# First two channel tiles' shift and scale by TensorE, and x loaded first, in a planned encoder layer

## Chip, cores, metric

One Trainium2 chip, one of its cores. The metric is the device time of one execution in microseconds (us): the median of the runs shown.

## What is computed

One encoder layer on x of 512 x 2048, in float32. A conditioning vector c gives six rows (shift, scale and gate for each half) through a 2048 x 12288 matrix `w_ada`:

```
c_act = silu(c)
sh1, sc1, gt1, sh2, sc2, gt2 = split(c_act @ w_ada + b_ada, 6)
h = rmsnorm(x, g_mix) * (1 + sc1) + sh1
proj = h @ w_in                                  # 2048 x 3072
y = concat(lru(proj[:1024]) * gelu(proj[1024:2048]), pool(proj[2048:])) @ w_out
x = x + gt1 * y
h = rmsnorm(x, g_ffn) * (1 + sc2) + sh2
x = x + gt2 * ((silu(h @ w_gate) * (h @ w_up)) @ w_down)
out = rmsnorm(x, g_final)
```

The change touches the first three lines: shift and scale of the first half, and the normalised, transposed x.

## The kernel before

The channels (2048) lie in 16 tiles of 128 partitions, the 512 frames along the free axis. x comes as 16 pieces of 128 frames x 512 channels (`xs`). ScalarE (ACT) squares each piece with a running sum; VectorE (DVE) and ACT make `rstd1` of the sums (`rstd_from`). Then ACT multiplies each piece by its rstd, TensorE (PE) transposes it in 128x128 blocks against the identity, and ACT copies the four blocks of a channel tile from PSUM into `xt[k]`. All 16 tiles are transposed in one loop, ahead of the rest of the program text.

Shift and scale of a chunk of channel tiles come from `ada_columns(which, k0, nk)`. The chunks are ADA_CHUNKS, tiles 0 and 1 alone, then seven pairs. SP loads the columns of `w_ada`, DVE multiplies each block by its entry of `c_act` and adds it up (`ada_fma`, 16 operations for a chunk), and a matmul of one column against ones sums over the partitions. DVE adds the bias from `cols_a` and writes `gs` (scale) and `sh` (shift). `shifted(k)` applies them on ACT and splits the result into a high and a low fp32r part, `h[k]`; ACT makes `hi`, DVE the difference `lo`. The projection follows with three matmuls for each product (hi.hi, hi.lo, lo.hi): six output tiles are held in PSUM (`held_job`, banks `acc`), the others are computed for tiles 0 and 1, 2 to 7 and 8 to 15 at a time (`group_job`, banks `mm`, of which there are two).

The order is not that of the text. A class `Program` records every operation, and `schedule` places them engine by engine after a cost model, by due times that `deadlines` derives; every engine and queue then runs its list in order. An operation with `lead` gets a due time ahead of all others, in the order of these numbers. Buffers come from pools: `blk` has 69 tiles of 128x512, `raw` six and `araw` four of 128x1024. `buffers` decides whether an operation may take a new one yet. Since every operation is issued from one helper, all have one line, L356 (L359 after the change), and are told apart by the names of their tiles: `araw<-in_w_ada` is a load of w_ada, `b<-araw,c_act,b` a multiply-add of `ada_fma`, `mm<-ones,b` the sum over partitions.

Of the kernel before, what the change touches and what calls it, by code (L numbers as in the profile page):

```python
# [36 lines left out]
class Program:  # L37
# [116 lines left out]
    def deadlines(self):  # L154

        at = 0.0
        users, order, serves = {}, {}, {}
        for op in self.ops:
            op["due"] = 1e9
            if op["q"] == "PE":  # L160
                op["due"] = op["nominal"] = at
                at += op["t"]
            for name in op["tiles"]:
                tag = self.tags[name]
                if name not in users and tag != "blk":
# [12 lines left out]
        for js in before:  # L178
            for j in js:
                behind[j] += 1  # L180
        latest, queued, held = [at + 50.0] * len(self.ops), {}, {}
        heap = [(-latest[i], -i) for i, n in enumerate(behind) if not n]
        heapq.heapify(heap)
        while heap:
            _, i = heapq.heappop(heap)
            op = self.ops[i := -i]
            q, due = op["q"], latest[i]
            tag = self.tags.get(op["w"][0][0]) if q == "SP" and op["w"] else None
            if tag in ("raw", "araw"):
                due = queued[tag] = min(due, queued.get(tag, 1e9) - 0.6)  # L190
            op["due"] = min(op["due"], due - op["t"] - (self.SLACK if not op["dma"] else self.SLACK_DMA if q == "SP" else self.SLACK_SUM))
            if q in ("DVE", "ACT", "SP"):
                t = max(op["t"], self.DMA_ISSUE) if q == "SP" else op["t"] * self.LOAD
                op["due"] = held[q] = min(op["due"], held.get(q, 1e9) - t)
            for j in before[i]:
                latest[j] = min(latest[j], op["due"])
                behind[j] -= 1
                if not behind[j]:
                    heapq.heappush(heap, (-latest[j], -j))
        for op in self.ops:  # L200
            if op["lead"] is not None:
                op["due"] = op["lead"] - 1e3 + 1e-4 * op["i"]

    def schedule(self):
# [22 lines left out]
        taken, last_use = set(), {}  # L227
        waiting, ready = [len(op["pred"]) for op in ops], [0.0] * len(ops)
        clock = {q: 0.0 for q in self.QUEUES.values()}
        dma_free, table, busy, port = 0.0, None, {}, 0.0  # L230
        start, left = [None] * len(ops), len(ops)
        pace = [op for op in ops if op["q"] == "PE"][::-1]
        shift, wide = 0.0, False
# [45 lines left out]
        while left:  # L279
# [4 lines left out]
            for (q, _), heap in lanes.items():  # L284
                now, tried = clock[q], []
                while heap and (wide or len(tried) < self.SCAN):
                    due, i = heapq.heappop(heap)
                    tried.append((due, i))
                    if q == "PE" and pace and ops[i]["nominal"] > pace[-1]["nominal"] + self.AHEAD:
                        continue  # L290
                    need, when = buffers(ops[i], now)
                    if when is None:
                        continue
                    t = max(now, ready[i], when, port if ops[i]["port"] else 0.0)
                    cand = (t, due + 2.0 * (ops[i]["table"] not in (None, table)), i, need)
# [21 lines left out]
                early[tag].append(place[name])  # L317
            start[i] = t
            if op["dma"]:
                issue = self.DMA_ISSUE if q == "SP" else self.DMA_BUILD  # L320
                clock[q] = t + issue
                dma_free = max(dma_free, t + issue + self.DMA_START - self.DMA_ISSUE) + op["t"]
                end = dma_free + self.DMA_LAND
            else:
                if op["table"] not in (None, table):
                    t, table = t + self.TABLE_LOAD, op["table"]
                    start[i] = t
                end = t + op["t"]
# [31 lines left out]
def hybrid_trunk(ctx: ExitStack, tc: tile.TileContext, a: dict, out: bass.AP):  # L360
# [58 lines left out]
    def rows_of(src):  # L419
        return src.rearrange("(r p) -> r p", p=P)  # L420

    rows_c = blk()[0:16, 0:P]
    nc.sync.dma_start(out=rows_c, in_=rows_of(a["c"][0]), lead=1)
    c_act = const.tile([P, KD], F32, name="c_act")
    tp = mmps()
    nc.tensor.transpose(out=tp[:, 0:16], in_=rows_c, identity=ident[0:16, 0:16])
    nc.scalar.activation(out=c_act, in_=tp[:, 0:16], func=AF.Silu)

    def param_columns(cols, rows, srcs, lead=None):
        r = 0  # L430
# [32 lines left out]
    for q in range(4):  # L463
        for t in range(NT):
            xs[t][q] = blk()
            nc.sync.dma_start(out=xs[t][q], in_=x2[t * P:(t + 1) * P, q * 512:(q + 1) * 512], lead=(0, 2, 4, 6)[q])
            ss = ss1[:, 4 * t + q:4 * t + q + 1]
            nc.scalar.activation(out=blk(), in_=xs[t][q], func=AF.Square, accum_out=ss)

    rstd1 = rstd_from(ss1, NT, after=sqrt_ready)  # L470
    xt = []
    for k in range(KD):
        ps = mmps("acc")
        for t in range(NT):
            if k % 4 == 0:
                nc.scalar.activation(out=xs[t][k // 4], in_=xs[t][k // 4], func=AF.Copy, scale=rstd1[:, t:t + 1])
            nc.tensor.transpose(out=ps[:, t * P:(t + 1) * P], in_=xs[t][k // 4][:, (k % 4) * P:(k % 4 + 1) * P], identity=ident)
        xt.append(blk())
        nc.scalar.activation(out=xt[k], in_=ps, func=AF.Copy)

# [25 lines left out]
    def ada_columns(which, k0, nk):  # L506

        nc_ = nk * P
        acc = blk()[:, 0:2 * nc_]
        nko = 512 // nc_  # L510
        for ko in range(0, KD, nko):
            w = nc.tile(pool, [P, 1024], F32, "araw", f"araw{next(ids)}").rearrange("p (s a b) -> p s a b", s=2, a=nko)
            for i in range(2):
                nc.sync.dma_start(out=w[:, i], in_=w_ada[:, ko:ko + nko, 3 * which + i, k0 * P:k0 * P + nc_],
                                  lead=5 if which + k0 == 0 else None)
            for i in range(nko):
                ada_fma(acc.rearrange("p (s b) -> p s b", s=2), w[:, :, i, :], ko + i)
# [187 lines left out]
    def pool_group(g):  # L705
# [485 lines left out]
```

## Time and profile before

| | |
|---|---|
| median of 3 runs | 1891.26 us (1891.05 to 1896.01) |
| profiled execution | 1895.01 us |
| its span, first to last instruction | 1893.1 us |
| PE busy | 1806.1 us, 95% |
| DVE busy | 1539.7 us, 81% |
| ACT busy | 936.4 us, 49% |
| moved by DMA | 429.97 MB, mean 227 GB/s |
| mean granted TensorE clock | 0.989 |

Times in the trace count from the first instruction. Matmuls overlap, so how far apart they start says more than their length. In the stretches, PEclk is the granted share of TensorE's clock (1.00 is 2.4 GHz, 0.5 is 1.2 GHz), and the DMA share is the mean busy share of the 16 DMA engines; since packets overlap it can pass 1.

### The profile page before, as it was taken

The numbers are of one execution on the slowest core, as the hardware profiler recorded it, in microseconds if no ns is written. First come the engines' busy times: TensorE is split into PE (matmuls) and PEld (weight loads), VectorE is DVE, ScalarE is ACT, GpSimd is POOL, SyncE is SP. The second block draws the span as 40 slices with busy tenths as digits, with TensorE's granted clock in tenths as the row PEclk, the third lists the DMA queues.
The fourth block names the chain that finished last, engine by engine and source line by source line (L and its number), as shares of the span: only waits on it lengthen the run. The fifth ranks groups of instructions, "written<-read, shape, count | busy, mean of one in ns | idle before, by whom it ended". The sixth has DMA issues, their size and how long they took to land.

```text
span 1893.1 us, 22786 instructions
## 1 busy us (share of the span) xinstructions
PE 1806.1 (95%) x8011; PEld 1473.2 (78%) x8011; DVE 1539.7 (81%) x1974; ACT 936.4 (49%) x1221; POOL 197.4 (10%) x192
## 2 busy tenths in 40 slices
PE   3899999899999999999999999999999999999996
PEld 2687877688887888888888788787887888888875
DVE  5898998889969878678787867877667887888888
ACT  7434684422377545454554544545445543333345
POOL 0000054500001111111111111111110000000011
PEclk9999999999999999999999999999999999999999
DMA  9999755499954778788868877876799765947566
GB/s 297 312 349 292 237 183 178 141 327 318 364 168 97 189 201 222 202 211 219 226 180 217 224 191 208 221 194 183 169 291 341 245 232 186 354 143 261 195 155 164
DMA packets 285763, 429.97 MB, mean 227 GB/s; under 512 B 20760, under 2 KB 119760, under 8 KB 285648
## 3 DMA queue, kind: packets, MB, share of 16 engines
q1 hardware_dynamic: 259408, 378.17, 59.9%
q0 software_dynamic: 26240, 50.34, 15.9%
q8 instruction: 63, 1.03, 0.2%
q14 instruction: 52, 0.43, 0.1%
HBM read 378.63 MB, written 49.81 MB: 226 GB/s over the span
## 4 chain that ended last, share of the span: by engine, by line
PE 64%; DVE 14%; DMA 9%; issue 8%; ACT 3%; POOL 1%; SPq 1%; ACTq 0%; DVEq 0%; POOLq 0%
PE acc L356 62%; DVE b L356 10%; DVE lo L356 4%; DMA araw<-in_w_ada 3%; PE mm L356 2%; ACT b L356 2%; DMA raw<-in_w_ada 1%; ACT hi L356 1%; DMA raw<-in_w_ffn_up 1%; DMA araw<-in_w_ffn_up 1%; SPq L356 1%; DMA araw<-in_w_ffn_gate 1%; DMA raw<-in_w_out 0%; DMA f<-b 0%; DMA raw<-in_w_in 0%
## 5 line engine op out<-in xcount | busy, mean ns | idle before, releaser
L356 PE MATMUL acc<-hi,b 128*128 128x512 f32 x4208 | 1271.4, 392 | 5.3 <-ACT hi L356 2.2
L356 PEld LDWEIGHTS acc<-hi,b 128*128 128x128 f32 x4208 | 789.6, 189 | 169.8 <-ACT hi L356 7.6
L356 PE MATMUL acc<-lo,b 128*128 128x512 f32 x2104 | 782.9, 393 | 4.4 <-DVE lo L356 4.3
L356 ACT ACTIVATE hi<-raw 128x1024 fp32r<-128x1024 f32 (+2 forms) x297 | 306.6, 1035 | 447.2 <-PE acc L356 362.5
L356 DVE TENSOR_TENSOR lo<-raw,hi 128x1024 fp32r<-128x1024 f32 (+2 forms) x297 | 356.1, 1202 | 148.4 <-ACT hi L356 144.1
L356 PEld LDWEIGHTS acc<-lo,b 128*128 128x128 f32 x2104 | 396.1, 189 | 91.5 <-DVE lo L356 10.9
L356 ACT ACTIVATE hi<-araw 128x1024 fp32r<-128x1024 f32 x264 | 279.7, 1060 | 283.1 <-PE acc L356 257.5
L356 DVE TENSOR_TENSOR lo<-araw,hi 128x1024 fp32r<-128x1024 f32 x198 | 241.5, 1220 | 58.2 <-ACT hi L356 57.5
L356 DVE SCALAR_TENSOR_TENSOR b<-araw,c_act,b 128x512 f32<-128x512 f32 (+1 forms) x315 | 232.0, 741 | 11.3 <-DMA araw<-in_w_ada 8.0
L356 DVE TENSOR_TENSOR b<-b,b 128x512 f32<-128x512 f32 (+4 forms) x318 | 194.3, 633 | 13.7 <-ACT b L356 11.3
L356 PE MATMUL acc<-b,hi 128*128 128x512 f32 x608 | 191.4, 400 | 5.0 <-ACT b L356 2.1
L356 ACT ACTIVATE b<-b 128x512 fp32r<-128x512 f32 (+2 forms) x223 | 128.6, 597 | 106.1 <-DVE b L356 64.9
L356 PEld LDWEIGHTS acc<-b,hi 128*128 128x128 f32 x608 | 115.9, 192 | 32.4 <-ACT b L356 4.3
L356 PE MATMUL acc<-b,lo 128*128 128x512 f32 x304 | 116.7, 398 | 2.5 <-DVE lo L356 2.5
L356 POOL DMA_DIRECT2D araw<-in_w_ffn_up x44 | 53.1, 1206 | 586.7 <-DVE lo L356 412.1
L356 ACT ACTIVATE b<-acc 128x512 f32<-128x512 f32 x142 | 82.1, 594 | 57.6 <-PE acc L356 42.6
L356 DVE SCALAR_TENSOR_TENSOR lo<-araw,hi 128x1024 fp32r<-128x1024 f32 x66 | 80.5, 1220 | 34.4 <-ACT hi L356 34.1
L356 DVE TENSOR_TENSOR araw<-araw,raw 128x1024 f32<-128x1024 f32 x88 | 106.7, 1219 | 0.8
L356 POOL DMA_DIRECT2D raw<-in_w_ffn_up x44 | 53.0, 1204 | 317.7 <-DVE lo L356 290.2
L356 DVE SCALAR_TENSOR_TENSOR araw<-araw,raw 128x1024 f32<-128x1024 f32 x66 | 79.9, 1219 | 6.9 <-DMA raw<-in_w_ffn_down 3.5
L356 PE MATMUL mm<-b,hi 128*128 128x512 f32 x192 | 62.1, 404 | 10.3 <-ACT b L356 10.3
L356 PEld LDWEIGHTS acc<-b,lo 128*128 128x128 f32 x304 | 58.5, 192 | 16.0 <-DVE lo L356 3.8
(72 smaller groups left out, 868.2 us busy)
## 6 DMA issues: line engine op xcount, KB each, us to landing
araw<-in_w_ada SPq DMA_DIRECT2D x256, 256.0 KB, 4.7
raw<-in_w_ffn_down SPq DMA_DIRECT2D x88, 512.0 KB, 5.3
f<-b SPq DMA_DIRECT2D x154, 256.0 KB, 3.7
b<-f SPq DMA_DIRECT2D x154, 256.0 KB, 6.0
araw<-in_w_ffn_gate SPq DMA_DIRECT2D x44, 512.0 KB, 3.8
raw<-in_w_ffn_up SPq DMA_DIRECT2D x44, 512.0 KB, 4.5
araw<-in_w_ffn_up POOLq DMA_DIRECT2D x44, 512.0 KB, 6.6
raw<-in_w_ffn_gate SPq DMA_DIRECT2D x44, 512.0 KB, 4.9
```

The lines of the kernel that those rows point to most:

```text
L356: getattr(getattr(self.nc, queue), method)(*args, **kw)
```

## The change

1. Tiles 0 and 1: `ada_scalars` takes the place of the multiply-adds. Each w_ada block is the stationary operand of a one-column matmul with `c_act`, 16 for the shift and 16 for the scale, adding up in PSUM. Four loads of 0.5 MB take the place of eight of 0.25 MB.
2. The rows of c, b_ada and the norms' gains are loaded from ACT's queue, not SP's. The planner counts them there.
3. x: the leads are 0, 2, 4 and 4.5 in place of 0, 2, 4 and 6, while tile 0's w_ada has 5; so all of x stands ahead of w_ada on SP.
4. `transposed(k)` makes one tile of `xt`, and the main loop calls it two tiles ahead of the chunk. For tiles 0 to 7 the moving operand is the identity times rstd (`diag`), a plain f32 matmul, and ACT does not scale x; for tiles 8 to 15 it stays as it was. The PSUM bank comes from `mm`, not `acc`.
5. The planner asks for buffers at the later of the engine's own clock and the latest start placed so far (`today`).

```diff
+XT_AHEAD = 2
+DIAG_TILES = 8
...
-                t = max(op["t"], self.DMA_ISSUE) if q == "SP" else op["t"] * self.LOAD
+                t = max(op["t"], self.DMA_ISSUE) if q == "SP" else self.DMA_ISSUE if op["dma"] else op["t"] * self.LOAD
...
-                    need, when = buffers(ops[i], now)
+                    need, when = buffers(ops[i], max(now, today))
...
+            today = max(today, t)
...
-    nc.sync.dma_start(out=rows_c, in_=rows_of(a["c"][0]), lead=1)
+    nc.scalar.dma_start(out=rows_c, in_=rows_of(a["c"][0]), lead=1)
...
-            nc.sync.dma_start(out=xs[t][q], in_=x2[t * P:(t + 1) * P, q * 512:(q + 1) * 512], lead=(0, 2, 4, 6)[q])
+            nc.sync.dma_start(out=xs[t][q], in_=x2[t * P:(t + 1) * P, q * 512:(q + 1) * 512], lead=(0, 2, 4, 4.5)[q])
...
-    for k in range(KD):
-        ps = mmps("acc")
+    diag = blk()
+    for t in range(NT):
+        ts(out=diag[:, t * P:(t + 1) * P], in0=ident, scalar1=rstd1[:, t:t + 1], scalar2=None, op0=ALU.mult)
+    def transposed(k):
+        ps = mmps()
         for t in range(NT):
+            tok, x = slice(t * P, (t + 1) * P), xs[t][k // 4]
+            if k < DIAG_TILES:
+                nc.tensor.matmul(ps[:, tok], x[:, (k % 4) * P:(k % 4 + 1) * P], diag[:, tok], start=True, stop=True)
+                continue
             if k % 4 == 0:
-                nc.scalar.activation(out=xs[t][k // 4], in_=xs[t][k // 4], func=AF.Copy, scale=rstd1[:, t:t + 1])
+                nc.scalar.activation(out=x, in_=x, func=AF.Copy, scale=rstd1[:, t:t + 1], after=xt[1])
...
+        if which == 0 and nk == 1:
+            return ada_scalars(k0)
...
+    def ada_scalars(k0):
+        ps = mmps()
+        for i in range(2):
+            for ko in range(0, KD, 8):
+                w = stage("araw", 8, P)
+                nc.sync.dma_start(out=w, in_=w_ada[:, ko:ko + 8, i, k0 * P:(k0 + 1) * P], lead=5 if k0 == 0 else None)
+                for k in range(8):
+                    nc.tensor.matmul(ps[:, i:i + 1], w[:, k, :], c_act[:, ko + k:ko + k + 1], start=ko + k == 0, stop=ko + k == KD - 1)
+        ada_end(0, k0, 1, ps)
...
     for ci, nk in enumerate(ADA_CHUNKS):
+        end = start + nk
+        for k in range(len(xt), min(KD, end + XT_AHEAD)):
+            transposed(k)
         ada_columns(0, start, nk)
```

What it does to the order, at three places. First, PE at the first projection matmuls, before (acc_138 and acc_140 are transposed tiles, acc_156 the first held output tile, b_171 and b_172 the two parts of channel tile 0):

```order
L356 MATMUL acc_140<-ident,b_97 128x128
L356 MATMUL acc_138<-ident,b_103 128x128
L356 MATMUL acc_140<-ident,b_99 128x128
L356 MATMUL acc_140<-ident,b_101 128x128
L356 MATMUL acc_140<-ident,b_103 128x128
L356 MATMUL acc_156<-b_171,hi_174 128x512
L356 MATMUL acc_156<-b_172,hi_174 128x512
L356 MATMUL acc_156<-b_171,lo_175 128x512
```

and now (mm_138 is a transposed tile with the diagonal b_118, mm_152 tile 1's shift and scale, acc_125 to 127 held output tiles):

```order
L359 MATMUL mm_138<-b_118,b_83 128x128
L359 MATMUL mm_152<-c_act,araw_153 128x1 x8
L359 MATMUL mm_138<-b_118,b_85 128x128
L359 MATMUL mm_138<-b_118,b_87 128x128
L359 MATMUL mm_152<-c_act,araw_154 128x1 x8
L359 MATMUL acc_125<-b_145,hi_148 128x512
L359 MATMUL acc_125<-b_146,hi_148 128x512
L359 MATMUL acc_125<-b_145,lo_149 128x512
L359 MATMUL mm_152<-c_act,araw_155 128x1 x8
L359 MATMUL acc_126<-b_145,hi_148 128x512
```

Before, 48 of the 64 transposes stood ahead of the first projection matmul; now 12 do, and the small matmuls of tile 1's first two loads stand there too.

Second, DVE ahead of `gs` of tiles 8 and 9, before (mm_355 is the sum for these tiles, b_406 the multiply-adds for tiles 14 and 15):

```order
L356 TENSOR_TENSOR lo_362<-raw_360,hi_361 128x1024
L356 SCALAR_TENSOR_TENSOR b_386<-araw_394,c_act,b_386 128x512
L356 SCALAR_TENSOR_TENSOR b_406<-araw_408,c_act,b_406 128x512
L356 TENSOR_TENSOR lo_365<-raw_363,hi_364 128x512
L356 SCALAR_TENSOR_TENSOR b_386<-araw_394,c_act,b_386 128x512
L356 TENSOR_TENSOR gs_154<-mm_355,cols_a 128x2
```

and now (mm_346 and b_405 in their places):

```order
L359 TENSOR_TENSOR lo_356<-raw_354,hi_355 128x512
L359 SCALAR_TENSOR_TENSOR b_385<-araw_393,c_act,b_385 128x512
L359 SCALAR_TENSOR_TENSOR b_405<-araw_406,c_act,b_405 128x512
L359 TENSOR_TENSOR b_188<-b_327,b_188 128x512
L359 TENSOR_TENSOR gs_123<-mm_346,cols_a 128x2
```

The `gs` stood behind the second w_ada load of tiles 14 and 15 (araw_408, the first is araw_407); now it stands behind their first (araw_406).

Third, PE at the second pooling group's first matmuls, before (mm_614 and mm_617 are its outputs, acc_624 a gate tile at channel tiles 12 and 13):

```order
L356 MATMUL acc_624<-b_398,hi_636 128x512
L356 MATMUL acc_624<-b_399,hi_636 128x512
L356 MATMUL mm_614<-b_603,hi_612 128x512
L356 MATMUL mm_617<-b_603,hi_612 128x512
L356 MATMUL acc_624<-b_398,lo_637 128x512
```

and now (mm_613, mm_616; acc_623 and 624 the same two gate tiles, at channel tiles 4 to 7):

```order
L359 MATMUL acc_623<-b_255,lo_630 128x512
L359 MATMUL acc_624<-b_229,lo_630 128x512
L359 MATMUL mm_613<-b_602,hi_611 128x512
L359 MATMUL mm_616<-b_602,hi_611 128x512
L359 MATMUL acc_624<-b_231,hi_629 128x512
```

The pooling matmuls stand 38 matmuls of 512 columns further up.

## Rows read from the trace of the kernel before

**Rows 1.** The page, parts 1 and 2: busy time; DMA in 40 slices.

```profile
PE 1806.1 (95%) x8011; PEld 1473.2 (78%) x8011; DVE 1539.7 (81%) x1974; ACT 936.4 (49%) x1221; POOL 197.4 (10%) x192
```

**Rows 2.** Stretches: busy time of each engine, clock, DMA share, GB/s.

```profile
core 0: us, PE busy (x) PEld busy (x) DVE busy (x) ACT busy (x) POOL busy (x), PEclk, DMA share, GB/s
0.00:10.00 10.00, 0.26 (x1) 0.18 (x1) 0.54 (x3) 6.50 (x14) 3.09 (x24) 1.00 0.70 212
...
40.00:50.00 10.00, 8.68 (x39) 5.77 (x38) 9.52 (x14) 10.00 (x20) 0.00 (x0) 0.83 0.92 286
50.00:60.00 10.00, 7.28 (x26) 5.25 (x27) 8.00 (x12) 2.00 (x3) 0.00 (x0) 0.89 0.93 298
...
130.00:140.00 10.00, 10.00 (x46) 8.28 (x45) 10.00 (x19) 3.25 (x5) 0.00 (x0) 1.00 1.05 370
...
150.00:160.00 10.00, 8.59 (x27) 6.84 (x28) 8.15 (x15) 6.15 (x11) 0.00 (x0) 0.66 0.85 276
...
250.00:260.00 10.00, 7.02 (x32) 5.53 (x31) 10.00 (x13) 9.91 (x12) 7.33 (x6) 1.00 0.73 239
```

**Rows 3.** Timeline of ACT: start, length, operation, count, idle time before and its releaser.

```profile
22.79 0.63 ACT L356 ACTIVATE b<-b 128x512 f32<-128x512 f32 x1 [5.98 <-DMA b<-in_x]
...
26.36 0.63 ACT L356 ACTIVATE b<-b 128x512 f32<-128x512 f32 x1
```

**Rows 4.** Timeline of SP's DMA queue.

```profile
5.13 0.97 SPq L356 DMA_DIRECT2D b<-in_b_ada  x2
...
8.71 2.37 SPq L356 DMA_DIRECT2D b<-in_x  x4
...
18.36 2.07 SPq L356 DMA_DIRECT2D b<-in_x  x4
...
83.21 2.94 SPq L356 DMA_DIRECT2D araw<-in_w_ada  x4
```

**Rows 5.** Timeline of DVE.

```profile
18.07 7.78 DVE L356 SCALAR_TENSOR_TENSOR b<-araw,c_act,b 128x256 f32<-128x256 f32 x15
...
29.25 0.15 DVE L356 SCALAR_TENSOR_TENSOR s<-s,s 128x4 f32<-128x4 f32 x1
...
92.40 1.40 DVE L356 SCALAR_TENSOR_TENSOR b<-araw,c_act,b 128x512 f32<-128x512 f32 x2
...
94.35 0.16 DVE L356 TENSOR_TENSOR gs<-mm,cols_a 128x2 f32<-128x2 f32 x1
...
146.41 0.75 DVE L356 SCALAR_TENSOR_TENSOR b<-araw,c_act,b 128x512 f32<-128x512 f32 x1 [0.85 <-DMA araw<-in_w_ada]
...
148.34 0.15 DVE L356 TENSOR_TENSOR gs<-mm,cols_a 128x2 f32<-128x2 f32 x1
```

**Rows 6.** Timeline of PE.

```profile
41.54 1.20 PE L356 MATMUL acc<-b,hi 128*128 128x512 f32 x2
...
97.38 1.43 PE L356 MATMUL acc<-b,hi 128*128 128x512 f32 x5
...
147.29 0.39 PE L356 MATMUL mm<-b,lo 128*128 128x512 f32 x1
151.41 2.92 PE L356 MATMUL acc<-b,hi 128*128 128x512 f32 x6 [1.68 <-ACT b L356]
...
154.99 0.63 PE L356 MATMUL acc<-b,lo 128*128 128x512 f32 x1
155.42 0.63 PE L356 MATMUL acc<-b,hi 128*128 128x512 f32 x1
```

**Rows 7.** Groups by form, 0 to 50 us (PE) and 78 to 148 us (DVE): busy, mean ns, idle.

```profile
L356 PE MATMUL acc<-ident,b 128*128 128x128 f32 x64 | 12.0, 340 | 5.6 <-ACT b L356 5.4
...
L356 PE MATMUL mm<-ones,b 128*128 128x1 f32 x8 | 1.6, 303 | 13.9 <-DVE b L356 13.9
...
L356 DVE SCALAR_TENSOR_TENSOR b<-araw,c_act,b 128x512 f32<-128x512 f32 x58 | 42.8, 747 | 1.9 <-DMA araw<-in_w_ada 1.8
```

**Rows 8.** Timeline of PE, later.

```profile
256.90 1.38 PE L356 MATMUL acc<-b,b 128*128 128x512 f32 x5 [2.98 <-DVE b L356]
...
379.33 0.79 PE L356 MATMUL mm<-b,hi 128*128 128x512 f32 x1 [4.30 <-ACT b L356]
```

More of the change, by code (lines that the diff above doesn't have):

```diff
@@ L229, in schedule @@
         clock = {q: 0.0 for q in self.QUEUES.values()}
-        dma_free, table, busy, port = 0.0, None, {}, 0.0
+        dma_free, table, busy, port, today = 0.0, None, {}, 0.0, 0.0
         start, left = [None] * len(ops), len(ops)
@@ L319, in schedule @@
             if op["dma"]:
-                issue = self.DMA_ISSUE if q == "SP" else self.DMA_BUILD
+                issue = self.DMA_BUILD if q == "POOL" else self.DMA_ISSUE
                 clock[q] = t + issue
@@ L427, in hybrid_trunk, with param_columns @@
     nc.scalar.activation(out=c_act, in_=tp[:, 0:16], func=AF.Silu)
-    def param_columns(cols, rows, srcs, lead=None):
+    def param_columns(cols, rows, srcs, queue, lead=None):
         r = 0
@@ L433, in param_columns @@
             n = src.shape[0]
-            nc.sync.dma_start(out=rows[r:r + n, :], in_=src, lead=lead)
+            queue.dma_start(out=rows[r:r + n, :], in_=src, lead=lead)
             r += n
@@ L471, in hybrid_trunk @@
     xt = []
-    for k in range(KD):
-        ps = mmps("acc")
+    diag = blk()
[3 more added lines that the diff above has]
+        ps = mmps()
         for t in range(NT):
+            tok, x = slice(t * P, (t + 1) * P), xs[t][k // 4]
+            if k < DIAG_TILES:
+                nc.tensor.matmul(ps[:, tok], x[:, (k % 4) * P:(k % 4 + 1) * P], diag[:, tok], start=True, stop=True)
+                continue
             if k % 4 == 0:
-                nc.scalar.activation(out=xs[t][k // 4], in_=xs[t][k // 4], func=AF.Copy, scale=rstd1[:, t:t + 1])
-            nc.tensor.transpose(out=ps[:, t * P:(t + 1) * P], in_=xs[t][k // 4][:, (k % 4) * P:(k % 4 + 1) * P], identity=ident)
+                nc.scalar.activation(out=x, in_=x, func=AF.Copy, scale=rstd1[:, t:t + 1], after=xt[1])
+            nc.tensor.transpose(out=ps[:, tok], in_=x[:, (k % 4) * P:(k % 4 + 1) * P], identity=ident)
         xt.append(blk())
@@ L513, in ada_columns @@
             for i in range(2):
-                nc.sync.dma_start(out=w[:, i], in_=w_ada[:, ko:ko + nko, 3 * which + i, k0 * P:k0 * P + nc_],
-                                  lead=5 if which + k0 == 0 else None)
+                nc.sync.dma_start(out=w[:, i], in_=w_ada[:, ko:ko + nko, 3 * which + i, k0 * P:k0 * P + nc_])
             for i in range(nko):
@@ L520, in ada_columns, with ada_end @@
             nc.tensor.matmul(ps[:, j:j + 1], acc[:, j * P:(j + 1) * P], ones[:, 0:1], start=True, stop=True)
+        ada_end(which, k0, nk, ps)
+    def ada_scalars(k0):
[7 more added lines that the diff above has]
+        ada_end(0, k0, 1, ps)
+    def ada_end(which, k0, nk, ps):
         b0 = which * 32 + k0
@@ L735, in hybrid_trunk @@
                   [b_ada[0:32, :], b_ada[48:80, :], rows_of(a["g_norm_mix"][0]), rows_of(a["g_norm_ffn"][0])],
-                  lead=3)
+                  nc.scalar, lead=3)
     start = 0
@@ L739, in hybrid_trunk @@
     for ci, nk in enumerate(ADA_CHUNKS):
+        end = start + nk
+        for k in range(len(xt), min(KD, end + XT_AHEAD)):
+            transposed(k)
         ada_columns(0, start, nk)
-        end = start + nk
         for k in range(start, end):
@@ L746, in hybrid_trunk @@
                           [a["w_conv"][0].rearrange("i (r p) -> (i r) p", p=P), rows_of(a["b_conv"][0]), rows_of(a["b_rg_a"][0]),
-                           rows_of(a["b_rg_i"][0]), rows_of(a["lru_lambda"][0]), a["ls_pool"][0].rearrange("g (r p) -> (g r) p", p=P)])
+                           rows_of(a["b_rg_i"][0]), rows_of(a["lru_lambda"][0]), a["ls_pool"][0].rearrange("g (r p) -> (g r) p", p=P)], nc.sync)
             sp, spn = softplus()
```

## Prediction, before the changed kernel ran

> **What bounds the kernel now.** I read the page first, then the stretches, then single engines. The page [rows 1] says TensorE (PE) is busy for 95% of 1893.1 us, so a change at the start can win only what PE loses there. The stretches [rows 2] show where: in 0 to 10 us PE does nothing (0.26 us), in 40 to 60 it is 87% and 73% busy at a granted clock of 0.83 and 0.89, in 130 to 140 it is full, in 150 to 160 it has 0.66 of its clock, and in 250 to 260 it is idle for 3 us. The reader is to see two more columns: DMA is at a share of 0.92 to 1.05 in the three stretches between 40 and 140, and VectorE (DVE) at 8.0 to 10.0 of 10 us. So once the projection runs, three things are nearly full at a time, and PE's early gain must be carried by the other two.
>
> Why PE starts late: ScalarE (ACT) takes its last Square of x at 26.36 us, since the last quarter of x landed so late (5.98 us of waiting at 22.79) [rows 3]; SP issued that quarter at 18.36, behind eight pieces of w_ada [rows 4]. rstd is ready at 29.40 [rows 5], and PE's first projection matmul comes at 41.54 [rows 6].
>
> Two places later decide what an early start is worth. Channel tiles 6 and 7 start on PE at 97.38 [rows 6]; their scale `gs` was written by DVE at 94.35, at the end of an unbroken run of DVE work whose last w_ada pieces were issued at 83.21 [rows 4, 5]. Tiles 8 and 9 start at 151.41 after PE finished its earlier work at 147.68: their `gs` stood in DVE's queue until 148.34, behind a fused multiply-add that waited 0.85 us for a w_ada piece at 146.41 [rows 5, 6]. That hole is followed by matmuls 0.43 us apart in place of 0.23 (154.99 to 155.42; five in 1.43 us at 97.38).
>
> **The change part by part.** The sum is made against the profiled execution, 1895.0 us (span 1893.1); the median of the runs is 1891.3, 3.7 us lower, and I carry the difference over to it.
>
> *x first, small rows on ACT.* Sixteen pieces of 0.262 MB are 4.19 MB. In 0 to 10 us DMA moved 212 GB/s at a share of 0.70, so some 300 GB/s when full [rows 2]: 14 us and 2 us to begin, 16 us. From the last Square to rstd is 3.0 us (26.36 to 29.40), so rstd stands at about 19 instead of 29.4. Five row DMAs now stand ahead of ACT's first Square; two such on SP took 0.97 us [rows 4], so 2.4 us, before any x has landed: nothing. The first rows took SP from 5.13 to 8.71, when the next x piece was issued [rows 4]: 3.6 us at most for the stream. The Trainium skill ("DMA: Bandwidth & Descriptors", Issuing engines are not separate DMA queues) speaks against more than that: DMAs of all engines run on the same 16 engines, and a second issuer saves issue time only. By that rule the moved rows win no bandwidth, and the sum by it is the one I use: 1.5 us, half of the 3 us that DMA stood idle in the first stretch (the other half is its start); ends 0 and 3.6.
>
> *Tiles 0 and 1 by PE.* DVE loses 2 x 16 multiply-adds, twice 16/15 of 7.78 us [rows 5], 16.6 us, and gains four 128x128 scalings. DVE was waiting for DMA there, so this is worth nothing by itself; it gives DVE slack until about 150. PE gains 64 matmuls of one column at up to 0.303 us and loses 4 [rows 7]: 18 us, nearly all in time when PE waits for the next piece. Only the last 8 behind a landing count, 2.4 us, against 0.5 us for DVE's last add: 2 us on a path that is now 9 us shorter. In the new order (the first above) PE also holds 16 of tile 1's small matmuls ahead of the first projection matmul, so that one waits for the sixth w_ada load: 9.45 MB by the order of SP, at 0.31 MB/us and 2 us, 32.5 us. **PE starts 9 us earlier** (28 to 36 by rates of 0.37 and 0.28).
>
> *What is late next.* Counted over SP's rows, the last w_ada piece of tiles 6 and 7 stands at 26.44 MB before and 26.38 MB now; for tiles 14 and 15 it is 50.43 and 50.37. The same bytes through a stream that is full: tile 6 cannot come 9 us earlier. Tile 8's `gs` is behind 45.97 MB before (the waiting piece at 146.41) and 45.39 MB now, as the second order above shows: 0.58 MB at 0.34 MB/us is 1.7 us, and 1.5 us from the start of the stream. So `gs` comes 3.2 us earlier by DMA, and 1.6 us more since DVE has less ahead of it than before (it ran from 146.41 to 148.34 behind that piece; I leave 0.3 us of the 1.9): **4.8 us**. PE itself would be there earlier still: from 97.38 it needs 216 matmuls of 0.2275 us, 49.1 us, nine of which are now done before tile 6, and tile 6 comes about 2 us earlier, 95.5; so it arrives near 145 and waits 1.7 us or so, where it waited 3.7. In 250 to 260 a hole of 2.98 us left the granted clock at 1.00 [rows 2, 8]; after the 3.7 us of 147.68 to 151.41 it was 0.66. A hole of 1.7 us should keep it: 13 matmuls x 0.20 us, **2.6 us**.
>
> *Transposes moved into the full stretch.* Before, all 64 were over by 46 us. Now they are made two tiles ahead: 16, those of tiles 12 to 15, come after tile 8 has started, when PE is full. PE was busy 12.0 us with 64 of them [rows 7], 0.19 each; **3.2 us lost** (2 to 5.4, the mean of one being 340 ns). The 32 with a diagonal of rstd are f32 matmuls of a shape that the trace lacks; between 0.19 and 0.43 (the 512-column matmul at the low clock) they cost up to 8 us more, but stand ahead of tile 6's and 8's gates, where PE waits: nothing.
>
> *DVE after 150.* By tile 14's `gs` DVE has passed 55.61 MB now and 54.10 before: six w_ada pieces, 4.5 us of multiply-adds at 0.747 us [rows 7] done ahead. In 240 to 260 DVE is full and PE loses 2.98 us behind it [rows 8]: I take 2 us back (0 to 3).
>
> Sum: -4.8 - 2.6 + 3.2 - 2.0 = **-6.2 us**, 1888.8 for the profiled execution, 1885 as a median.
>
> **The rivals.** *A, the whole start is kept.* For it: 286 and 298 GB/s in 40 to 60 against 370 in 130 to 140 [rows 2] look like a stream held back by its buffers and by DVE, and DVE is now lighter. At 350 GB/s 26.4 MB would be in by 77.5, not 89; then PE's own work sets the pace. It keeps 9 us of start, 2.6 of clock and 2 of DVE, loses 3.2: -10.4, 1881 (1876 to 1883). Against it: shares of 0.92 and 0.93. The skill's ceiling of about 358 GB/s for one core (same page, Specifications) would allow it: by that figure alone, an estimate, 26.4 MB need 74 us.
>
> *B, nothing arrives.* DMA's first hole is not closed, the clock falls after the wait at tile 8 as before, the transposes cost 5 us: -1.7 - 1.6 - 2 + 5 = about 0, 1891 (1887 to 1893). For it: three resources full at a time, equal bytes.
>
> *C, slower: the pooling matmuls.* The new order puts the four pooling groups' first matmuls 10, 38, 30 and 23 places earlier among the 512-column matmuls (the third order above shows the second group). PE is in order, and before the fourth group it already waited 4.30 us for an ACT split [rows 8]. If the pooled tiles come no earlier than the rest of the kernel, the second group stalls 38 x 0.2275 = 8.6 us, and one fall of the clock adds 2.6: +11.2 on -6.2, 1896. It decides from 6.2 us of stall on. Against it: ACT's splits of these tiles were placed earlier too, and POOL's and DVE's part was over well before.
>
> *D, part of it does nothing:* if the first projection matmul is not earlier than 38 us, the order of PE eats the start; this ends as B.
>
> **How the numbers follow.** A measurement here tells 0.3%, 5.7 us, from no change: faster is below 1885.6. My forecast has 0.36 (its own range 1881 to 1888.5), A 0.26, B with D 0.26, C 0.12. Faster: all of A and 0.23 of the forecast, 0.49; slower: nearly all of C and a little of B's end, 0.13; the rest 0.38. The likeliest time is 1885. The range takes A down to 1875 and most of C, up to 1895.
>
> **What would show it.** Right: ACT's last Square near 16 and rstd near 19; first projection matmul at 30 to 35; tile 6 at 94 to 97 and tile 8 at 145 to 148, each right behind a `gs`; no low clock near 150; DMA full from 3 us on. A shows as tile 6 before 90. C shows as PE waits for ACT of over 5 us between 290 and 380. The forecast is wrong if tile 8 starts after 150, or if the gain at tile 8 is not there at 260.

## The result, and the profile after

The changed kernel takes 1902.11 us (median of 5 runs, 1901.52 to 1909.11) beside 1891.83 us for the kernel before (5 runs on the same chip). The ratio is **1.0063, 95% interval 1.0042 to 1.0083**: slower by 0.6%, where 1885 was forecast. The profiled execution took 1901.52 us, its span is 1899.7 us, 6.6 us more than before.

The page's busy line [rows 1] shows PE with 26.7 us more work and DVE with 10.0 us less:

```profile
PE 1832.8 (96%) x8163; PEld 1502.1 (79%) x8163; DVE 1529.7 (81%) x1946; ACT 931.5 (49%) x1214; POOL 194.4 (10%) x192
```

The stretches of the changed kernel, with the columns of [rows 2]:

```profile
0.00:10.00 10.00, 0.65 (x2) 0.36 (x2) 0.80 (x4) 5.41 (x11) 2.13 (x23) 1.00 0.69 170
10.00:20.00 10.00, 1.14 (x6) 1.17 (x6) 0.58 (x4) 9.30 (x27) 0.00 (x0) 1.00 1.09 383
20.00:30.00 10.00, 10.00 (x49) 10.00 (x48) 3.92 (x11) 2.21 (x3) 0.00 (x0) 1.00 1.10 378
30.00:40.00 10.00, 9.31 (x50) 8.89 (x49) 1.59 (x5) 2.01 (x3) 0.00 (x0) 1.00 0.80 258
40.00:50.00 10.00, 10.00 (x47) 9.13 (x47) 0.00 (x0) 0.60 (x1) 0.00 (x0) 0.59 0.47 146
50.00:60.00 10.00, 10.00 (x39) 8.95 (x38) 4.71 (x9) 4.00 (x6) 0.00 (x0) 0.56 0.37 117
...
110.00:120.00 10.00, 10.00 (x33) 8.20 (x34) 9.08 (x28) 2.56 (x4) 0.00 (x0) 0.66 1.09 360
...
150.00:160.00 10.00, 9.72 (x44) 7.42 (x42) 9.88 (x20) 3.82 (x7) 0.00 (x0) 1.00 1.03 345
...
250.00:260.00 10.00, 10.00 (x45) 8.27 (x45) 9.23 (x13) 8.71 (x12) 5.74 (x6) 1.00 0.58 181
```

For the same stretches before, three rows are needed beside those of [rows 2]:

```profile
10.00:20.00 10.00, 0.39 (x1) 0.18 (x1) 2.43 (x6) 5.65 (x16) 0.00 (x0) 1.00 0.99 289
20.00:30.00 10.00, 0.99 (x4) 0.93 (x4) 8.21 (x27) 4.27 (x11) 0.00 (x0) 1.00 1.02 324
30.00:40.00 10.00, 8.26 (x47) 6.66 (x47) 7.78 (x18) 10.00 (x19) 0.00 (x0) 1.00 1.09 369
```

Summed over these columns, 1.1 MB more than before have come in by 30 us. The loss is behind that, most of it in 40 to 60 us. DVE does nothing at all in the first of these stretches (9.52 us before), DMA falls to 146 and 117 GB/s (286 and 298 before): 3.2 MB less have come in by 60 us, 10 us of a stream of some 0.3 MB/us. PE is shown busy throughout, at a clock of 0.59 and 0.56. What PE does there is in its timeline (start, length, operation, records in the run, idle time before):

```profile
18.86 12.08 PE L359 MATMUL mm<-c_act,araw 128*128 128x1 f32 x56 [12.26 <-DMA araw<-in_w_ada]
...
38.00 2.11 PE L359 MATMUL mm<-c_act,araw 128*128 128x1 f32 x16
39.98 0.69 PE L359 MATMUL mm<-b,b 128*128 128x128 f32 x4
40.51 2.23 PE L359 MATMUL mm<-c_act,araw 128*128 128x1 f32 x16
42.60 1.20 PE L359 MATMUL acc<-b,hi 128*128 128x512 f32 x2
43.60 0.63 PE L359 MATMUL acc<-b,lo 128*128 128x512 f32 x1
44.03 3.41 PE L359 MATMUL mm<-c_act,araw 128*128 128x1 f32 x16
...
50.00 3.41 PE L359 MATMUL mm<-c_act,araw 128*128 128x1 f32 x16
```

Each one-column f32 matmul leaves two records, so the eight of one w_ada piece are a run of 16: 3.41 us where the granted clock is 0.50, 2.11 and 2.23 us in the two runs that lie mostly where it is 1.00. At 1.00 the records start 0.112 us apart, at 0.50 0.213 us. The first 56 records, 12.08 us, are 0.213 us apart too. The clock column prints 1.00 there, but the trace has no clock record before 38.39 us; by the spacing PE ran at the low clock. The group by form over 0 to 60 us has all 64 matmuls as 128 records:

```profile
L359 PE MATMUL mm<-c_act,araw 128*128 128x1 f32 x128 | 24.9, 325 | 12.3 <-DMA araw<-in_w_ada 12.3
```

DVE's timeline shows who waits for them. `gs` of tile 0 waits 6.40 us for PE, that of tile 1 waits 16.10 us, and the first multiply-add of tiles 2 and 3 stands right behind it in DVE's list:

```profile
20.53 0.16 DVE L359 SCALAR_TENSOR_TENSOR s<-s,s 128x4 f32<-128x4 f32 x1
...
33.96 0.16 DVE L359 TENSOR_TENSOR gs<-mm,cols_a 128x1 f32<-128x1 f32 x1 [6.40 <-PE mm L359]
...
36.65 0.69 DVE L359 TENSOR_TENSOR b<-b,b 128x512 fp32r<-128x512 f32 x1
53.45 0.16 DVE L359 TENSOR_TENSOR gs<-mm,cols_a 128x1 f32<-128x1 f32 x1 [16.10 <-PE mm L359]
...
53.72 0.48 DVE L359 TENSOR_SCALAR b<-araw,c_act 128x512 f32<-128x512 f32 x1
...
111.24 0.16 DVE L359 TENSOR_TENSOR gs<-mm,cols_a 128x2 f32<-128x2 f32 x1 [0.88 <-PE mm L359]
...
164.60 0.15 DVE L359 TENSOR_TENSOR gs<-mm,cols_a 128x2 f32<-128x2 f32 x1
```

SP's queue shows the stream standing still behind both: seven of the eight pieces of tiles 0 and 1 are issued by 29.26, the eighth at 33.95 and none until 40.15, for lack of a free buffer.

```profile
12.71 6.04 SPq L359 DMA_DIRECT2D araw<-in_w_ada  x4
...
22.85 6.78 SPq L359 DMA_DIRECT2D araw<-in_w_ada  x3
29.72 1.05 SPq L359 DMA_DIRECT2D raw<-in_w_in  x2
33.95 0.37 SPq L359 DMA_DIRECT2D araw<-in_w_ada  x1
34.41 0.53 SPq L359 DMA_DIRECT2D raw<-in_w_in  x1
40.15 15.75 SPq L359 DMA_DIRECT2D araw<-in_w_ada  x10
```

PE's runs on the four pieces of tile 1 end at 40.11, 42.74, 47.44 and 53.41 (start and length above); SP goes on with w_ada at 40.15, 42.77, 47.47 and 53.44, each time within 0.04 us. So a piece is issued when PE lets go of a buffer. What lands in these buffers then waits for DVE until 53.72.

From there the delay is carried by the same links that the prediction followed. `gs` of tiles 6 and 7 is written at 111.24, not 94.35 [rows 5], that of tiles 8 and 9 at 164.60, not 148.34; tile 8 starts on PE at 167.68, 16.3 us later than before [rows 6]:

```profile
109.36 1.84 PE L359 MATMUL mm<-ones,b 128*128 128x1 f32 x8 [4.51 <-DVE cols_b L359]
...
167.68 1.75 PE L359 MATMUL acc<-b,hi 128*128 128x512 f32 x4 [1.82 <-ACT b L359]
...
328.79 0.79 PE L359 MATMUL acc<-b,lo 128*128 128x512 f32 x1 [4.56 <-DVE lo L359]
...
366.40 0.73 PE L359 MATMUL mm<-b,hi 128*128 128x512 f32 x2 [1.66 <-ACT b L359]
...
388.32 0.50 PE L359 MATMUL mm<-b,hi 128*128 128x512 f32 x1 [3.02 <-ACT b L359]
```

Later work gives part of it back. Counted along PE, the 1250th 512-column matmul starts 18.8 us later than before, the 1350th 11.4, the 2300th 7.9, and the end comes 6.6 us later. Around the first two lies the fourth pooling group, for which the kernel before waited 4.30 us [rows 8] and then had the low clock from 378.7 to 385.5. The changed kernel waits 3.02 us there, at 388.32, and keeps its clock.

### The profile page after: what moved, and what is told of

Same layout as the page of the kernel before. It is cut to its first block, busy times and chain, and to the rows that moved or that the text cites. A ratio compares the mean times of both kernels' runs of the same rounds, so it can differ in the third digit from the quotient of the medians.

```text
span 1899.7 us, 23048 instructions
## 1 busy us (share of the span) xinstructions
PE 1832.8 (96%) x8163; PEld 1502.1 (79%) x8163; DVE 1529.7 (81%) x1946; ACT 931.5 (49%) x1214; POOL 194.4 (10%) x192
## 4 chain that ended last, share of the span: by engine, by line
PE 68%; DVE 12%; DMA 10%; issue 6%; ACT 2%; SPq 0%; POOL 0%; DVEq 0%; ACTq 0%; POOLq 0%
PE acc L359 64%; DVE b L359 8%; PE mm L359 4%; DVE lo L359 3%; DMA araw<-in_w_ada 3%; DMA f<-b 3%; ACT b L359 1%; DMA b<-f 1%; DMA raw<-in_w_ffn_down 1%; DMA raw<-in_w_ffn_gate 1%; ACT hi L359 1%; DVE araw L359 1%; DMA b<-in_x 1%; DMA araw<-in_w_ffn_up 0%; SPq L359 0%
## 5 line engine op out<-in xcount | busy, mean ns | idle before, releaser
L359 DVE SCALAR_TENSOR_TENSOR b<-araw,c_act,b 128x512 f32<-128x512 f32 x285 | 217.1, 767 | 6.2 <-DMA araw<-in_w_ada 3.6
L359 DVE TENSOR_TENSOR b<-b,b 128x512 f32<-128x512 f32 (+5 forms) x318 | 192.2, 625 | 15.4 <-ACT b L359 10.1
L359 ACT ACTIVATE b<-acc 128x512 f32<-128x512 f32 x126 | 73.6, 593 | 68.6 <-PE acc L359 46.7
L359 DVE TENSOR_TENSOR b<-acc,b 128x512 f32<-128x512 f32 x94 | 61.4, 684 | 11.5 <-PE acc L359 11.4
```

The lines of the kernel that those rows point to most:

```text
L359: getattr(getattr(self.nc, queue), method)(*args, **kw)
```

## The experiments

**The theories.** *H1*: the 64 one-column matmuls on PE hold up DVE, the four w_ada buffers and so the stream; in form *H1a* it is the order (the planner prices such a matmul at 0.107 us), in form *H1b* the PE time itself. *H2*: the transposes two tiles ahead and the f32 matmuls with the diagonal cost PE the time. *H3*: x ahead of w_ada delays w_ada. *H4*: the planner's new rule (`today`) orders the later part worse. Every kernel is planned anew, so a few us between two of them may be the planner's; conclusions rest on larger differences or on the rows at the place. All ratios are against the kernel before, run beside each:

| kernel | median us | ratio, 95% interval | `gs` of tiles 6, 7 | `gs` of tiles 8, 9 |
|---|---|---|---|---|
| before | 1891.83 | | 94.35 | 148.34 |
| changed | 1902.11 | 1.0063 (1.0042, 1.0083) | 111.24 | 164.60 |
| e1 tiles 0, 1 by DVE | 1896.87 | 1.0016 (1.0004, 1.0029) | 93.11 | 148.74 |
| e4 tile 0 by PE | 1897.27 | 1.0026 (1.0010, 1.0042) | 97.89 | 153.92 |
| e5 a quarter of the matmuls | 1890.04 | 0.9983 (0.9967, 1.0000) | 91.06 | 144.41 |
| e3 price 0.43 us | 1930.89 | 1.0195 (1.0177, 1.0214) | 126.88 | 179.81 |
| e8 six w_ada buffers | 1928.53 | 1.0188 (1.0166, 1.0210) | 100.44 | 152.03 |
| e8b the same, kernel before | 1928.61 | 1.0198 (1.0176, 1.0220) | 90.04 | 139.88 |
| e13 changed, 8 ahead | 1906.92 | 1.0079 (1.0050, 1.0109) | 114.30 | 166.78 |
| e11 e1 with 8 ahead | 1884.60 | 0.9963 (0.9948, 0.9977) | 92.65 | 143.18 |
| e6 e1 with all 16 first | 1895.60 | 1.0006 (0.9992, 1.0020) | 91.46 | 145.61 |
| e14 e11, diagonal for 4 | 1883.96 | 0.9953 (0.9934, 0.9973) | 93.01 | 145.06 |
| e16 e11, old loads | 1888.69 | 0.9987 (0.9966, 1.0008) | 96.07 | 147.75 |

**Is it the matmuls?** e1 takes the branch out of `ada_columns` (tile 0's loads keep their lead of 5), e4 keeps it for tile 0 alone, e5 keeps it and multiplies 2 of 8 k-steps of each piece, so the sums lack the other six.

```diff
 e1  -        if which == 0 and nk == 1:
     -            return ada_scalars(k0)
 e4  -        if which == 0 and nk == 1:
     +        if which + k0 == 0:
 e5  -                for k in range(8):
     +                for k in (0, 4):
```

> The changed kernel with the shift and scale of tiles 0 and 1 by VectorE again; x first, small rows on ScalarE's queue, transposes two tiles ahead and the diagonal all stay. H1 (the one-column matmuls of tiles 0 and 1 on PE hold up VectorE, its w_ada buffers and the stream): VectorE's 16 us wait for PE near 53 is gone, DMA's share stays over 0.8 from 40 to 60, tile 6 starts PE at 94 to 99 instead of 112, and the time is 1883 to 1892. H2 (transposes ahead and the diagonal's f32 matmuls cost PE the time): tile 6 may move, but the time stays at 1898 to 1904. H3 (x ahead of w_ada delays w_ada): tile 6 stays after 106 and the time at 1898 to 1904. H4 (the planner's new rule orders the later part worse): 1898 to 1903, with tile 6 early and the loss found after 300.

> The changed kernel with tile 0 alone by one-column matmuls on PE, tile 1 by VectorE again: 32 of them in place of 64, some 14 us of PE instead of 27. H1: VectorE's wait for the sums is 0 to 6 us in place of 16.1, tile 6 starts PE between 94 and 104, and the time lies between that of both tiles by VectorE and that of the changed kernel, 1884 to 1896. H2, H3, H4: 1898 to 1904, as the changed kernel.

> The changed kernel with a quarter of the one-column matmuls: of each w_ada piece of tiles 0 and 1 the k-steps 0 and 4 alone go through PE, 16 matmuls in place of 64, so that the shift and scale of these two tiles sum over 4 of 16 k-steps only (that part is left out). The pieces are all still loaded, and VectorE's work is that of the changed kernel. H1b (PE's 27 us for the 64 matmuls is what holds the w_ada buffers): first projection matmul at 30 to 36, VectorE's wait for PE under 6 us, tile 6 before 99, time 1884 to 1896. If instead it is the path by PE as such (pieces by halves, order of the queue), tile 6 stays after 106 and the time at 1898 to 1904. H2, H3 and H4 also give 1898 to 1904.

e1: DVE's wait is gone. Its first multiply-add of tiles 2 and 3 comes at 40.17 (53.72 in the changed kernel) and stands ahead of `gs` of tile 1; PE's first projection matmul is at 32.76:

```profile
40.17 0.49 DVE L359 TENSOR_SCALAR b<-araw,c_act 128x512 f32<-128x512 f32 x1 [0.28 <-DMA araw<-in_w_ada]
...
44.54 0.15 DVE L359 TENSOR_TENSOR gs<-mm,cols_a 128x1 f32<-128x1 f32 x1
...
93.11 0.16 DVE L359 TENSOR_TENSOR gs<-mm,cols_a 128x2 f32<-128x2 f32 x1 [0.19 <-PE mm L359]
```

```profile
32.76 2.08 PE L359 MATMUL acc<-b,hi 128*128 128x512 f32 x7 [0.69 <-ACT b L359]
```

The place came out as H1 expected, the total 5 us above its range: some of the loss is later (below). In e4 DVE waits 6.62 us for PE, and the total is 1 us above its range. e5 loads every piece as the changed kernel does and has DVE do no more; 48 matmuls are missing. Its `gs` of tiles 6 and 7 stands 20.2 us earlier and it is 12 us faster, with PE's group down to a quarter:

```profile
L359 PE MATMUL mm<-c_act,araw 128*128 128x1 f32 x32 | 5.8, 285 | 13.8 <-DMA araw<-in_w_ada 13.8
```

No matmul, 32 and 64 of them give 93.11, 97.89 and 111.24, more than in proportion. **H1 holds; H2, H3 and H4 alone fall**, since all their parts are in e5. H1a and H1b are not parted by it: in e5's plan two multiply-adds of tiles 2 and 3 stand ahead of tile 1's `gs`, in the changed kernel none.

**Order or PE time?** e3 gives the planner the price that the trace shows at the low clock, for every f32 matmul, those with the diagonal too.

```diff
-            return max(0.107, stream), stream
+            return max(0.107 if args[1].dtype == F32R else 0.43, stream), stream
```

> The changed kernel in which only the planner's price of an f32 matmul is 0.43 us (what the trace shows at the low clock) in place of 0.107; the work is the same, its order may differ. H1a (the loss is a wrong order: VectorE's adds for tile 1 stand in its queue ahead of the multiply-adds of tiles 2 and 3 since the planner believes the sums to come 20 us earlier): VectorE's wait of 16.1 us for PE falls under 6, tile 6 starts before 104, and the time is 1886 to 1895. H1b (the 27 us of matmul time on PE itself is the loss, and no order hides it): tile 6 at 108 to 114 and 1898 to 1905. H2, H3, H4: 1898 to 1905.

It is slower still. The planner now puts 12 multiply-adds of tiles 2 and 3 ahead of tile 1's `gs` (69.56), but these wait for w_ada, the first until 54.72, since PE still holds the buffers; PE ends tile 1's sums at 59.7 and soon waits 8.67 us for that `gs`:

```profile
54.72 0.49 DVE L359 TENSOR_SCALAR b<-araw,c_act 128x512 f32<-128x512 f32 x1 [2.35 <-DMA araw<-in_w_ada]
...
59.85 3.12 DVE L359 SCALAR_TENSOR_TENSOR b<-araw,c_act,b 128x512 f32<-128x512 f32 x4 [3.86 <-DMA araw<-in_w_ada]
```

So a higher price alone cures nothing, and H1a in this form falls. But the total is also far above H1b's range (1898 to 1905): the new order costs something of its own. That no other order could help is not shown.

**The buffers.** e8 is the changed kernel with six w_ada buffers, paid for with four general blocks; e8b the kernel before with the same.

```diff
-BUFS = {"blk": 69, "raw": 6, "araw": 4, "hi": 3, "lo": 3, "acc": 6, "mm": 2}
+BUFS = {"blk": 65, "raw": 6, "araw": 6, "hi": 3, "lo": 3, "acc": 6, "mm": 2}
```

> The changed kernel with six w_ada buffers in place of four (and 65 general blocks in place of 69). H1 by its second link (the stream stops since the four buffers are held while VectorE waits 16 us): two more buffers are 1.05 MB more, 3 to 3.5 us of stream, so tile 6 starts 3 to 5 us earlier, 107 to 109, and the time is 1896 to 1900, unless the four blocks less cost more. If the stream is not held by buffers: tile 6 at 111 to 114, 1900 or more.

> A control for the run with six w_ada buffers: the kernel before with the same buffers (six for w_ada, 65 general blocks). If the 33 us that this run lost after the 1500th matmul come from the four blocks less, this kernel loses 25 to 40 us in the same stretch, 1915 to 1932. If they came from the changed start, it stays at 1888 to 1898. At the start it should gain little, 0 to 3 us at tile 6, since VectorE was never held there.

At tile 6 e8 is 10.8 us ahead of the changed kernel (111.24 to 100.44), more than twice what was expected, e8b 4.3 us ahead of the kernel before. That fits held buffers, but not they alone: in e8's plan the first multiply-adds of tiles 2 and 3 come at 39.61, ahead of tile 1's `gs` at 52.81, so buffers and order changed together. That PE's held buffers stop the stream is shown by the times of SP's issues above. The total says nothing of it: both lose 35 to 37 us after PE's 1500th matmul (e8 goes from 2.4 us ahead of the kernel before to 33.1 behind, e8b from 3.9 ahead to 33.2 behind), with the changed start and without it.

**The four combinations.** e11 and e13 set XT_AHEAD to 8 without and with the matmuls on PE, e6 to 16 without.

```diff
-XT_AHEAD = 2
+XT_AHEAD = 8
```

> Tiles 0 and 1 by VectorE, transposes eight tiles ahead. H2 in its small form: 2 to 4 us under the run with two ahead (1896.87), 1889 to 1894. If hidden: 1895 to 1899. Against the kernel with all 16 at the start (1895.6) nothing is expected, 0 to 2 us less.

> The changed kernel, tiles 0 and 1 by PE, with transposes eight tiles ahead in place of two. With it the two parts stand in all four combinations (tiles by PE or VectorE, two or eight ahead). H1b: the loss at the start stays, tile 6 after 106 and DMA idle between 36 and 58, and only what the transposes of tiles 12 to 15 cost after the 400th matmul is gained: 1892 to 1900, that is 8 to 15 us over the form by VectorE with eight ahead (1884.6). If what that form gained was from the transposes alone, 1884 to 1890.

> Tiles 0 and 1 by VectorE, as in the run that undid this part alone (1896.87, ratio 1.0016), and all 16 channel tiles of x transposed at the start as before the change (8 with the diagonal, 8 plain) in place of two ahead. H2 in its small form (16 transposes of tiles 12 to 15 in PE's full stretch cost 3 to 5 us, which are the steps of +4 between the 400th and the 1050th matmul there): 1890 to 1894, and PE's lead over the kernel before stays between the 400th and the 650th matmul. If the transposes are hidden where they are: no change, 1895 to 1899; a worse start by up to 4 us is possible too, since 40 more transposes stand ahead of tile 2.

By DVE, eight ahead in place of two wins 0.5% (1.0016 to 0.9963), more than expected; by PE it wins nothing (1.0063 to 1.0079). In e13 DVE's `gs` of tile 1 waits longer than in the changed kernel, and DMA all but stops:

```profile
40.00:50.00 10.00, 10.00 (x72) 9.49 (x70) 0.00 (x0) 3.21 (x6) 0.00 (x0) 0.93 0.09 22
```

```profile
57.56 0.16 DVE L359 TENSOR_TENSOR gs<-mm,cols_a 128x1 f32<-128x1 f32 x1 [18.37 <-PE mm L359]
```

So between e11 and e13 the matmuls on PE, with the plan made for them, are worth 22 us of median; e13's range ended at 1900. H2's small form shows between PE's 400th and 650th 512-column matmul: with 16 transposes in there e1 falls back by 3.7 us against the kernel before, e6 without them by 0.2, e11 gains 1.1. e6's total, expected at 1890 to 1894, is not told apart from e1's.

**A mixed form** takes the first of the four k-steps of each piece on PE and leaves three to DVE, two ahead (e9) and eight ahead (e10).

```diff
+            if split:
+                for j in range(2):
+                    nc.tensor.matmul(ps[:, j:j + 1], w[:, j, 0, :], c_act[:, ko:ko + 1], start=ko + j == 0, stop=False)
-            for i in range(nko):
+            for i in range(split, nko):
```

> The changed kernel with tiles 0 and 1 shared: of each w_ada piece, which holds four k-steps of both halves, PE takes the first k-step by one-column matmuls (16 for the two tiles, plus the 4 that add up VectorE's part), VectorE the other three. Nothing is left out. H1b (the loss was PE time of 64 such matmuls holding the buffers): tile 6 at 93 to 98, time 1887 to 1895. If any such matmul among the first pieces costs the start: tile 6 after 103, over 1898.

> As the shared form, with transposes eight tiles ahead in place of two, so that those of tiles 12 to 15 stand before tile 8. H2 in its small form: PE keeps its lead between the 400th and the 650th matmul (in the run with tiles 0 and 1 by VectorE and two ahead it lost 3.7 us there, with all 16 at the start 0.2), so 2 to 4 us less than the shared form, 1884 to 1892. If those transposes are hidden: the same as the shared form.

e9: 1893.52, ratio 1.0012 (1.0001, 1.0023); e10: 1894.45, 1.0015 (1.0000, 1.0030). Not better than DVE alone, and with eight ahead 0.5% worse than e11: even 16 such matmuls win nothing. e10's range, 1884 to 1892, was missed.

**Diagonal, and x first.** e14 has DIAG_TILES = 4, e16 the loads of the kernel before.

```diff
 e14 -DIAG_TILES = 8
     +DIAG_TILES = 4
 e16 -    nc.scalar.dma_start(out=rows_c, in_=rows_of(a["c"][0]), lead=1)
     +    nc.sync.dma_start(out=rows_c, in_=rows_of(a["c"][0]), lead=1)
     -lead=(0, 2, 4, 4.5)[q])
     +lead=(0, 2, 4, 6)[q])
     -                  nc.scalar, lead=3)
     +                  nc.sync, lead=3)
```

> The best form so far (tiles 0 and 1 by VectorE, transposes eight ahead, 1884.6, ratio 0.9963) with the diagonal for four tiles in place of eight. If the f32 matmuls with the diagonal cost PE time that counts, 2 to 5 us less; if the diagonal only replaces ScalarE's scaling off the path, the same within 3 us: 1882 to 1888, and a later order made by the planner may move it by as much again.

> The best form so far (1884.6) with the loads of the kernel before: last quarter of x behind the first w_ada pieces, small rows on SP's queue. If x first is what gives PE its earlier start: rstd at 28 to 30, first projection matmul after 40 in place of 37.6. If that start is worth the time (H1's reading of the start), 1888 to 1894. If the start is lost at the w_ada stream anyway (tile 6 within 2 us of the form with x first, 94), the same as there: 1882 to 1888.

e14 is the same as e11. e16's first projection matmul comes at 38.04, e11's at 37.58, but its `gs` of tiles 6 and 7 3.4 us later, and its ratio is 0.2% higher, with intervals that overlap: x first, with the rows on ACT's queue, seems to be worth 2 to 4 us, through the stream and not through PE's start; that is not settled.

**Without the planner's rule.** e2 is the kernel before with `ada_scalars` alone, e7 is e1 with the rule taken back.

```diff
 e7  -                    need, when = buffers(ops[i], max(now, today))
     +                    need, when = buffers(ops[i], now)
```

> The kernel before with one part of the change alone: shift and scale of tiles 0 and 1 by one-column matmuls on PE; x, rows, transposes and the planner's rules as before. H1: VectorE waits over 8 us for PE's sums before its multiply-adds of tiles 2 and 3, tile 6 starts PE after 105 (97.4 before), and the time is 1897 to 1906. H2, H3 and H4: none of their parts is in it, so 1888 to 1894, with tile 6 at 97 or before, since VectorE has 16 us less to do.

> Tiles 0 and 1 by VectorE (as in the run at 1.0016), with the planner's new rule on when a buffer counts as free taken back, so that the order of everything after the start may be another. H4 (the rule costs the later part): 1888 to 1893, with the gain after the 300th matmul. If the rule helps, 1899 or more. If it does nothing: 1895 to 1899.

e2: 1951.53 us, 1.0302 (1.0280, 1.0325); e7: 1940.49, 1.0255 (1.0229, 1.0281). Both stop PE for over 50 us (53.99 before 185.41, 57.89 before 171.84), whoever does tiles 0 and 1. In e7 SP issues 62 loads of w_ada in a row from 100 us on, before the weights that PE waits for:

```profile
171.84 1.22 PE L359 MATMUL mm<-b,hi 128*128 128x512 f32 x2 [57.89 <-ACT hi L359]
```

```profile
100.22 64.94 SPq L359 DMA_DIRECT2D araw<-in_w_ada  x62
165.21 1.29 SPq L359 DMA_DIRECT2D raw<-in_w_rg_i  x2
166.60 5.93 SPq L359 DMA_DIRECT2D raw<-in_w_in  x6
```

So in these forms the rule is no cost but what keeps this order from happening (the kernel before, planned without it, has no such stop), and e2's total can't be read as the price of the matmuls. Its start can: DVE waits 19.18 and 7.65 us for PE's two sums, and `gs` of tiles 6 and 7 is at 106.86, as H1 said.

## Why the prediction was wrong

**The step that failed** is the one that put the small matmuls where they cost nothing: "PE gains 64 matmuls of one column at up to 0.303 us and loses 4 [rows 7]: 18 us, nearly all in time when PE waits for the next piece. Only the last 8 behind a landing count, 2.4 us." Two things are wrong in it.

- *The price.* The row of 8 in [rows 7] is 4 matmuls, since each leaves two records: 1.6 / 4 = 0.40 us, not 0.303. 64 of them are 25.6 us; measured 24.9, at 0.22 us where the clock is 1.00 and 0.43 where it is 0.50.
- *The cover.* A piece of 0.524 MB comes every 1.4 us at the 378 GB/s of 20 to 30 us, and PE needs 2.1 to 3.4 us for it. PE is the slower side, so it does not wait for pieces: pieces wait for PE. The prediction's own figures said so, 8 x 0.303 = 2.4 us for a piece against 0.524 / 0.31 = 1.7 us; the two rates were never put side by side. The Trainium skill (TensorE: Matmul & The Clock Gate, LDWEIGHTS (loading the stationary operand)) states that a weight load takes its time by its columns, 128 / 1.2 = 107 ns; two for each of 64 matmuls would be 13.7 us, an estimate from that page. The trace agrees where the granted clock is 1.00, with records 0.112 us apart, and shows twice that, 0.213 us, where it is 0.50.

What followed from it: DVE's list has tile 1's `gs` ahead of the next multiply-adds, so a late sum stops DVE (16.10 us); a stopped DVE frees no buffer; the stream that was to be "full from 3 us on" ran at 146 and 117 GB/s. The prediction counted DVE's 16.6 us as slack and never asked who is queued behind the add that now waits for PE.

Point by point:

- *x first, rstd at 19*: right in kind. ACT's last Square is at 18.55 (26.36 before; forecast near 16), rstd at 20.53 (29.25), 1.5 us later than forecast. The 1.5 us at the start of the stream come out in size: 5.5 MB by 20 us, against 5.0. The Trainium skill (DMA: Bandwidth & Descriptors, Issuing engines are not separate DMA queues) states that DMAs of all issuing engines run on the same 16 DMA engines. The trace does not speak against it: with rows on a second issuer 0 to 10 us moved 170 GB/s at a share of 0.69, against 212 at 0.70; no run moves the rows alone.
- *First projection matmul at 32.5*: wrong, 42.60. With the tiles on DVE it is 32.76 (e1), by another path than the one that was summed.
- *`gs` of tile 8 4.8 us earlier, the hole short, the clock kept*: wrong for the changed kernel (16.3 us later), by the prediction's own sign, tile 8 after 150. Two steps in it fail by themselves. From 95.5 us 207 matmuls of 0.2275 us end at 142.6, not "near 145", which leaves a hole of 4 us and not 1.7. And a short hole need not keep the clock: the changed kernel waits 1.82 us before 167.68, and the clock is 0.50 from 168.1 to 171.5. The nearest test of the rest is e5, where the matmuls cost little: that `gs` is 3.9 us earlier (144.41), but a wait of 2.03 us is followed by 0.50 from 147.6 to 151.0, and the span is 3.4 us shorter than before, not 6.2. In e1 that `gs` is not earlier (148.74). In e11 the forecast figures come out, 5.2 us earlier (143.18), a hole of 0.59 us at 146.25, the clock 1.00 in 150 to 160 and 1884.60 us, but partly by luck: DVE has its 16.6 us back there, and the 16 transposes are not in the full stretch.

```profile
147.48 2.00 PE L359 MATMUL acc<-b,hi 128*128 128x512 f32 x4 [2.03 <-ACT b L359]
```

- *16 transposes in the full stretch, 3.2 us*: right; 3.7 in e1, 2.7 in the changed kernel between the same two matmuls.
- *The diagonal, nothing*: right by e14, which is e11 with four such tiles fewer.
- *DVE after 150, 2 us*: the hole of 2.98 us [rows 8] is gone (PE 10.00 of 10 us in 250 to 260), but on a kernel that was 18 us late, so the term can't be told apart.
- *Rivals*: D named the point (no matmul before 38 us), but priced it as "ends as B", 1891, without a stall of the stream. A's ceiling of 358 GB/s is none here: 10 to 20 us moved 383. C's mechanism did not show: no PE wait for ACT of over 5 us between 290 and 380, the longest there being 4.56 us for DVE and 1.66 for ACT, and 3.02 just behind, at 388.32. Its 1896 and the range's 1895 were too low for a stall of the stream, which no rival had.

## What to carry to other kernels

When work moves to another engine, compare rates before sums: time for one buffer on the new engine against the time in which the stream fills one. Here the engine was slower, so the work did not hide in its waits; it held buffers. Everything that shares them or stands behind its result in an in-order list then stops too. And count records against instructions in the code before taking a price from a row.

The best forms measured keep these two tiles on DVE, load x first and transpose eight tiles ahead: 0.9963 (0.9948, 0.9977) with the diagonal for eight tiles and 0.9953 (0.9934, 0.9973) for four, faster than both kernels.

## What the runs showed of the hardware

A one-column f32 matmul with a 128x128 stationary operand costs 0.22 us where the granted clock is 1.00 (two records 0.112 us apart, 38.5 to 41.7 us) and 0.43 where it is 0.50, as much as a 512-column matmul of the fp32r kind there (0.43). The 128-column f32 matmuls with the diagonal are no further apart: 0.213 us in the run at 35.24, 0.112 in that at 39.98. Ahead of the first clock record of a trace (38.39 us in the changed kernel) the clock column's 1.00 is no measurement: the records of 18.86 to 30.80 are spaced as at 0.50. PE shown busy for 10.00 of 10 us does not mean the full clock: while it did these matmuls between short runs of the projection, the granted clock was 0.50 from 41.8 to 58.9 us, 17 us on end, where the kernel before had two falls of 3.4 us (40.8 to 44.2, 57.8 to 61.2) with PE less busy [rows 2].
